# Three halves of RMS-norm factors spread over the partitions by a trip through DRAM instead of four TensorE transposes, in a hybrid attention and gated-MLP layer

## The chip, the cores and the metric

One Trainium2 chip, one core. The metric is the time of one execution in microseconds (us), the median of three runs. The work is spread over TensorE (PE, its weight loads PEld), VectorE (DVE), ScalarE (ACT), GpSimd (POOL) and SyncE (SP). DMAs are issued from two queues, SP's and ACT's; an engine that issues a DMA runs its instructions in order, so a DMA that waits holds what is behind it on that engine.

## The reference

One encoder layer on x of 1024 tokens by 1024 features, all float32:

```python
hn = rmsnorm(h, norm_mix)
qa, ka, va, qb, kb, vb = split(hn @ w_in)
o_a = window_gqa_sink(rope(qa), rope(ka), va, sink)     # |i-j| <= 128, 8 heads, 2 kv heads
o_b = neighbourhood_attention(qb, kb, vb, rpb)          # 8 heads, window 8 x 16 on a 16 x 64 grid
mix = concat(rmsnorm(o_a, norm_a), rmsnorm(o_b, norm_b))
h = h + mix @ w_out
hn = rmsnorm(h, norm_ffn)
h = h + (silu(conv3(hn @ w_gate) + conv_b) * (hn @ w_up)) @ w_down
return rmsnorm(h, norm_final)
```

Here `rmsnorm(y, g) = y * rsqrt(mean(y*y) + eps) * g`, with the mean over the features of one token.

## The kernel before

Activations lie transposed: features on the 128 partitions, tokens along the free dimension, in tiles of 128 by 1024 that are worked on as two halves of 512 tokens (h = 0 and 1; `tsl(h)`). A float32 product is made of three TensorE matmuls over a high and a low part of each operand (`hi` by an ACT copy, `lo` by a DVE subtraction), so every weight and every activation that goes into a product passes once through ACT and once through DVE. The gate and up products of the MLP and its down product each use seven block products in place of eight (names `11`, `12`, `s1` to `s4`, `22`, and `t1` to `t4` for the other operand), and the weights' sums and differences are made on DVE (`ws`).

Since tokens lie along the free dimension, a norm needs one factor per column, equal on all partitions. Squares are added up over the tiles; `inverse_narrow` (or `add_up` and `inverse_root`) transposes the sum on PE, reduces it on DVE to `v`, 128 partitions by 4 columns, one value per token, takes the root on ACT and the reciprocal on DVE. `widen(v, tag)` then turns `v` into a 128 by 512 tile: four PE transposes, each of one column of `v` broadcast to 128 columns, into a PSUM bank `sw`. The product with the factor and the gain is a SCALAR_TENSOR_TENSOR on DVE. The change touches this step at three places, named so in the rest:

- Place A, the norm of attention A's output, second half. `wide_a(1)` at L847 to L851 widens and ACT copies the bank into the tile `rstda`; `normed_a` (L855) multiplies the four tiles `mixa`. These steps are hung on the project job (`aux[...]`) that PE runs between the attention steps.
- Place B, the norm of attention B's output, second half: the loop at L991 to L998, `mixb` times the bank, then the split into `mgh` and `mgl` for the output product.
- Place F, the MLP norm, first half. In the loop over (h, d) of the output product's second part, `inverse_narrow` stands after (1, 1) and `widen` within (1, 3). `settle_out` adds each finished bank to `h1` (DVE, L1063), spills it to DRAM from ACT's queue (`h1d`, L1064), squares it (ACT, L1067) and adds the squares (DVE, L1069). `normed(0, wide, K1)` (L1074) and `operand` (ACT L1050, DVE L1051: the tiles `hg`) make the MLP's operands, first of the tiles K1 = 0 to 3, then of K2 = 4 to 7. The first MLP products `units[0].p1`, `units[1].p1` read K1's, `units[0].p2` reads K2's.

Three things set the order. PE's is the order of the code (`manual_schedule`). On the other engines a scheduler orders the instructions, where `tc.high_priority` draws one forward, `behind(...)` holds one until a marked instruction has been placed, and data dependencies do the rest; each engine then runs its list strictly in order. And the buffers of a pool come free in turn. `head_weights(i, "s2")` (L1083 by `sub`) makes four weight differences `ws` for the first MLP units; nothing but their loads and the scheduler sets their place.

The last norm of the kernel already goes through memory, for its second half: `as_rows` (L1499 to L1503) transposes `v` once to 4 rows of 128, ACT copies them to SBUF, one DMA writes the 2 KB to DRAM and a second reads them back to all 128 partitions.

Of the kernel before, what the change touches and what calls it, by code (L numbers as in the profile page):

```python
# [13 lines left out]
F32 = mybir.dt.float32  # L14
F32R = mybir.dt.float32r
AF = mybir.ActivationFunctionType
ALU = mybir.AluOpType
PSUM = bass.MemoryType.PSUM

D, S, HD = 1024, 1024, 64  # L20
KT = D // 128
NB = S // 128
HALF = 512
# [29 lines left out]
C_NMIX, C_NFFN, C_NFIN, C_NA, C_NB, C_CW, C_CB, C_SINK = 0, 8, 16, 24, 28, 32, 98, 120  # L53
# [5 lines left out]
def hybrid_layer(tc, xT, w_first, w_in, w_out, w_gate, w_up, w_down, small, sink, rpb, consts, rope, out):  # L59
    nc = tc.nc  # L60
    with ExitStack() as ctx:
# [7 lines left out]
        tpool = inner("temps", 3)  # L69
        apool = inner("att", 2)  # L70
        spool = inner("stats", 6)

        slots = {"xg": 16, "op": 14, "mix": 8, "rstd": 1}

        def big(name, tag, dt=F32):
            return lpool.tile([128, S], dt, name=name, tag=tag, bufs=slots[tag])
# [4 lines left out]
        def bank(name, tag):  # L81
            return psum.tile([128, HALF], F32, name=name, tag=tag)

        f32 = lambda ap: ap.bitcast(F32)
        tsl = lambda h: slice(h * HALF, (h + 1) * HALF)
# [4 lines left out]
        col = lambda c: par[:, c:c + 1]  # L90
# [15 lines left out]
        for name, dst, n in (("h", his, 2), ("h", his, 2), ("l", los, 2), ("l", los, 2), ("w", None, 2)):  # L106
            t = flat(big(name, "mix", F32R)[:, :], n)
# [26 lines left out]
        ident = cst[:, K_ID:K_ID + 128]  # L134
# [17 lines left out]
        mark = {}  # L152

        def behind(*names):

            stack = ExitStack()
            for n in names:
                stack.enter_context(tc.issue_after(mark[n].ins))
            return stack
# [23 lines left out]
        def product(ps, ws, xs, h):  # L183

            for i, (w, x) in enumerate(zip(ws, xs, strict=True)):
                block(ps, w, x, h, i == 0, i == len(ws) - 1)
                yield
# [23 lines left out]
        def inverse_narrow(sqs, dim, tag, n=4):  # L211

            ps = bank("ss", tag)
            v = cpool.tile([128, n], F32, name="v4", tag="v4", bufs=4, padded_shape=[128, 4])
            if len(sqs) == 1:
                for c in range(n):
                    nc.tensor.transpose(ps[:, c * 128:(c + 1) * 128], sqs[0][:, c * 128:(c + 1) * 128], ident)
                with tc.high_priority(offset=500):
                    nc.vector.tensor_reduce(v, ps[:, 0:n * 128].rearrange("p (c w) -> p c w", w=128), axis=mybir.AxisListType.X, op=ALU.add)
                    mark["narrow root"] = nc.scalar.activation(v, v, AF.Sqrt, bias=eps, scale=1.0 / dim)  # L220
            else:
                for i, sq in enumerate(sqs):
                    for c in range(n):
                        nc.tensor.matmul(ps[:, c:c + 1], sq[:, c * 128:(c + 1) * 128], ones[:, 0:1], start=c == 0 and i == 0,
                                         stop=i == len(sqs) - 1, skip_group_check=True)
                with tc.high_priority(offset=500):
                    nc.scalar.activation(v[:, 0:n], ps[:, 0:n], AF.Sqrt, bias=eps, scale=float(D) / dim)
            with tc.high_priority(offset=500):
                mark["narrow"] = nc.vector.reciprocal(v[:, 0:n], v[:, 0:n])
            return v  # L230

        def widen(v, tag, n=4):

            wide = bank("sw", tag)
            for c in range(n):
                nc.tensor.transpose(wide[:, c * 128:(c + 1) * 128], v[:, c:c + 1].to_broadcast([128, 128]), ident)
            return wide
# [345 lines left out]
        mg, h1, norm = [None] * 8, [None] * KT, {"halves": 0}  # L583
# [81 lines left out]
        xg, first = [None] * KT, [Project(m) for m in range(3)]  # L665
# [58 lines left out]
        t = quarters(big("f", "mix"))  # L724
# [71 lines left out]
        aux = {}  # L796
# [48 lines left out]
        def wide_a(h):  # L845
            def go():
                if h == 0:  # L847
                    live["op"] += 1
                    norm["a"] = big("rstda", "op")
                with tc.high_priority(offset=500):  # L850
                    nc.scalar.activation(norm["a"][:, tsl(h)], widen(norm["v"][:, 4 * h:4 * h + 4], "pj"), AF.Copy)  # L851
            return go

        def normed_a(i, h):
            return lambda: nc.vector.scalar_tensor_tensor(  # L855
                mix[i][:, tsl(h)], mix[i][:, tsl(h)], col(C_NA + i), norm["a"][:, tsl(h)], op0=ALU.mult, op1=ALU.mult)

        aux[11, 8], aux[12, 2], aux[12, 5], aux[12, 11], aux[12, 13] = square_a, narrow_a, narrow_a, wide_a(0), wide_a(1)
        for i in range(8):
            aux[13, 1 + i + i // 2] = normed_a(*divmod(i, 2))  # L860
        aux[1, KEYS] = second_k
        filler = rest()
        live["op"] = sum(needs(m) for m in range(3))
# [1 line left out]
        def fill(n):  # L865
            while n > 0 and next(filler, False):
                n -= 1
# [3 lines left out]
        for g in range(2):  # L871
            for b in range(NB):
                q, t = unit_window(g, b)
# [59 lines left out]
        for u in range(len(flat)):  # L933
            q, t, need, kind = flat[u]
# [52 lines left out]
        with tc.high_priority(offset=500):  # L987
            vb2 = [inverse_narrow([last[:, tsl(h)]], 512, "pt") for h in range(2)]
        fill(4)
        mg[4:8] = [(big("mgh", "xg", F32R), big("mgl", "xg", F32R)) for _ in range(4)]  # L990
        for h in range(2):  # L991
            wide = widen(vb2[h], "pt")
            for i in range(4):
                x = mix[4 + i][:, tsl(h)]
                hi, lo = (t[:, tsl(h)] for t in mg[4 + i])
                nc.vector.scalar_tensor_tensor(x, x, col(C_NB + i), wide, op0=ALU.mult, op1=ALU.mult)
                nc.scalar.activation(hi, x, AF.Copy)
                nc.vector.tensor_tensor(lo, x, f32(hi), op=ALU.subtract)  # L998
            if h == 0:
                wo = [load_wo(d, True) for d in range(2)]  # L1000
                fill(3)
# [19 lines left out]
        def load_raw(src, n):  # L1021
            raw = fpool.tile([128, n, 128], F32, name="raw", tag="raw", bufs=3, padded_shape=[128, KT, 128])
            nc.sync.dma_start(raw, src)
            return raw
# [9 lines left out]
        def load_half(src):  # L1034

            t = half_raw()
            nc.sync.dma_start(t, src)
            return t
# [16 lines left out]
        K1, K2 = range(0, 4), range(4, 8)  # L1055
        B, W = {}, {}
        late, total = [], [None, None]
        at = lambda k, h: h1[k][:, tsl(h)]
# [12 lines left out]

        def normed(h, wide, ds):
            for d in ds:
                nc.vector.scalar_tensor_tensor(at(d, h), at(d, h), col(C_NFFN + d), wide, op0=ALU.mult, op1=ALU.mult)  # L1074

        def pure(f):
            raw = load_raw(w_gate[f], KT)
# [5 lines left out]
        sub = lambda o, x, y: nc.vector.tensor_tensor(o, x, y, op=ALU.subtract)  # L1083
# [5 lines left out]
        def head_weights(i, name):  # L1089
            f, t = FO[i], wsum[i]  # L1090
            if name == "s1":
                u = load_raw(w_up[f], KT)
                nc.vector.tensor_tensor(t, u[:, 0:4], u[:, 4:8], op=ALU.add)
            elif name == "s2":
                g = load_half(w_gate[f, :, 0:4])
                sub(t, t, g)
            elif name == "s4":
                g = load_half(w_gate[f, :, 4:8])
                sub(t, g, t)
            elif name == "s3":  # L1100
                g, u = load_half(w_gate[f, :, 0:4]), load_half(w_up[f, :, 0:4])
                sub(t, g, u)
            else:
                t = load_half(w_up[f, :, 4:8])
            W[f, name] = split_w(t, 4)

        for h in range(2):
            for d in range(KT):
                if h == 0 and d + 2 < KT:
                    wo.append(load_wo(d + 2, False))  # L1110
                ps = bank("pj", ("o", "s", "pj")[(h * KT + d) % 3])
                for step, _ in enumerate(product(ps, wo[d], mg[4:8], h)):
                    if (h, d, step) == (1, 3, 1):
                        wide = widen(v, "pt")
                late.append((d, h, ps))
                if h == 1 and d == 1:
                    v = inverse_narrow([total[0]], D, "pt")
                settle_out()
                if h == 0 and d in (3, 4):
                    pure((0, FT // 2)[d - 3])  # L1120
                if h == 0 and d >= 5 or h == 1 and d == 0:
                    head_weights((d - 5) % KT, "s1")
                if h == 1 and d == 3:
                    normed(0, wide, K1)
                    B[1, 1] = [operand(at(k, 0), "xg") for k in K1]
                if h == 1 and d == 4:
                    normed(0, wide, K2)
                    B[2, 1] = [operand(at(k, 0), "xg") for k in K2]
# [146 lines left out]
        v = inverse_narrow([total[1]], D, "pt")  # L1275
        units[1].p2()
        wide = widen(v, "pt")
# [194 lines left out]
        sq, todo, vs = {}, [], {}  # L1472
# [75 lines left out]
        for i, (p, j, c) in enumerate(order):  # L1548
# [10 lines left out]
            ps = banks[p, j]  # L1559
# [27 lines left out]
        for k, cols in enumerate(quarters):  # L1587
            for j in (2, 3):
                ps = banks[6, j]
# [17 lines left out]
        first = quarters[1].start  # L1607
# [98 lines left out]
```

## Time and profile before

| | us |
|---|---|
| median of 3 runs (lowest, highest) | 1014.76 (1014.33, 1014.77) |
| the profiled execution, its own time | 1014.52 |
| its span, first to last instruction | 1012.7 |
| PE busy | 1005.1 (99%) |
| DVE busy | 835.0 (82%) |
| ACT busy | 560.7 (55%) |

Times in the trace are counted from the start of the span; 1.8 us of the execution lie outside it. Rows of the timeline give start, duration, engine, line, operation, output and inputs, sizes, and in brackets the idle time of the engine ahead of the row with what ended it. Matmuls are pipelined, so their durations overlap; what one of them costs PE is read from the distance between starts.

### The profile page before, as it was taken

How to read it: one execution, taken by the hardware profiler on the slowest of the kernel's cores; microseconds unless marked ns; L12 is line 12 of the kernel's file. 1: busy time of each engine (PE TensorE's matmuls, PEld its weight loads, DVE VectorE, ACT ScalarE, POOL GpSimd, SP SyncE). 2: the span in 40 equal slices, each digit the busy share in tenths (PEclk: the TensorE clock that was granted, in tenths of full speed). 3: DMA queues.
4: the chain of work that ended last, by engine and by line, in shares of the span. 5: the costliest groups of instructions: out<-in, count | busy, mean ns of one | idle time of the engine just before them, and what ended most of it. 6: DMA issues, size and time to landing. Idle time of an engine off the chain costs nothing.

```text
span 1012.7 us, 14836 instructions
## 1 busy us (share of the span) xinstructions
PE 1005.1 (99%) x5083; PEld 889.5 (88%) x5083; DVE 835.0 (82%) x1570; ACT 560.7 (55%) x1079; POOL 101.9 (10%) x186
## 2 busy tenths in 40 slices
PE   9999999999999999999999999999999999999997
PEld 8899998999899888888888888888888888888887
DVE  7899887768888799999987786786777678996775
ACT  8468776658687554565544443444444645544451
POOL 0224342232232100000000000000000000000001
PEclk9999999999999999999999999999999999999999
DMA  8223122333334366232552333323232699866654
GB/s 295 83 76 92 32 73 63 84 84 84 83 94 136 126 203 222 74 103 64 200 185 92 107 115 115 105 94 119 100 127 84 236 333 318 305 233 238 213 168 177
DMA packets 68372, 145.20 MB, mean 143 GB/s; under 512 B 8260, under 2 KB 18760, under 8 KB 68296
## 3 DMA queue, kind: packets, MB, share of 16 engines
q1 hardware_dynamic: 58216, 119.01, 36.6%
q10 hardware_dynamic: 10080, 25.24, 6.4%
q8 instruction: 40, 0.66, 0.3%
q14 instruction: 36, 0.29, 0.1%
HBM read 103.85 MB, written 28.58 MB: 131 GB/s over the span
## 4 chain that ended last, share of the span: by engine, by line
PE 96%; ACT 1%; DVE 1%; DMA 1%; SPq 0%; issue 0%; DVEq 0%
PE pj L179 8%; PE pj L181 8%; PE pj L180 8%; PE x L1045 8%; PE x L1043 8%; PE x L1044 7%; PE dn L1045 7%; PE dn L1044 7%; PE dn L1043 7%; PE s L393 4%; PE y L1045 4%; PE y L1043 4%; PE y L1044 4%; PE pt L548 2%; PE pt L472 2%; PE z L1043 2%
## 5 line engine op out<-in xcount | busy, mean ns | idle before, releaser
L1043 PE MATMUL x<-hg,whi 128*128 128x512 f32 x352 | 133.5, 379 | 0.0
L1044 PE MATMUL x<-hg,whi 128*128 128x512 f32 x352 | 133.4, 379 | 0.0
L1045 PE MATMUL x<-hg,wlo 128*128 128x512 f32 x352 | 133.4, 379 | 0.0
L1043 PE MATMUL dn<-xd,whi 128*128 128x512 f32 (+1 forms) x330 | 120.8, 366 | 0.0
L1044 PE MATMUL dn<-xd,whi 128*128 128x512 f32 (+1 forms) x330 | 120.5, 365 | 0.0
L1045 PE MATMUL dn<-xd,wlo 128*128 128x512 f32 (+1 forms) x330 | 120.5, 365 | 0.0
L1017 ACT ACTIVATE whi<-ws 128x512 fp32r<-128x512 f32 (+1 forms) x100 | 60.8, 621 | 75.2 <-DVE ws L1157 14.5
L432 ACT ACTIVATE p<-p,nm 128x385 f32<-128x385 f32 (+3 forms) x128 | 75.0, 586 | 45.9 <-DVE nm L424 43.5
L179 PE MATMUL pj<-xgh,whi 128*128 128x512 f32 x245 | 99.7, 407 | 0.0
L436 POOL TENSOR_SCALAR p<-p,sm 128x384 f32<-128x384 f32 (+1 forms) x128 | 75.9, 606 | 195.2 <-DVE sm L434 178.1
L180 PE MATMUL pj<-xgl,whi 128*128 128x512 f32 x245 | 92.9, 379 | 0.0
L181 PE MATMUL pj<-xgh,wlo 128*128 128x512 f32 x245 | 92.9, 379 | 0.0
L1017 ACT ACTIVATE whi<-raw 128x512 fp32r<-128x512 f32 (+1 forms) x102 | 61.0, 611 | 49.9 <-PE x L1044 15.0
L1018 DVE TENSOR_TENSOR wlo<-ws,whi 128x512 fp32r<-128x512 f32 (+1 forms) x100 | 66.7, 680 | 20.0 <-ACT whi L1017 19.7
L447 DVE TENSOR_TENSOR pl<-pt,ph 128x384 fp32r<-128x384 f32 (+2 forms) x108 | 63.4, 587 | 17.1 <-ACT ph L446 16.0
L1043 PEld LDWEIGHTS x<-hg,whi 128*128 128x128 f32 x352 | 66.5, 189 | 9.4
L1044 PEld LDWEIGHTS x<-hg,whi 128*128 128x128 f32 x352 | 66.5, 189 | 9.4
L1045 PEld LDWEIGHTS x<-hg,wlo 128*128 128x128 f32 x352 | 66.5, 189 | 9.4
L1018 DVE TENSOR_TENSOR wlo<-raw,whi 128x512 fp32r<-128x512 f32 (+1 forms) x102 | 66.5, 668 | 5.8 <-ACT whi L1017 5.8
L1518 POOL TENSOR_TENSOR h<-h,wide 128x256 f32<-128x256 f32 x4 | 2.8, 731 | 671.3 <-ACT wide L1514 671.3
L446 ACT ACTIVATE ph<-pt 128x384 fp32r<-128x384 f32 (+2 forms) x108 | 55.3, 512 | 25.7 <-PE pt L472 14.5
L1043 PEld LDWEIGHTS dn<-xd,whi 128*128 128x128 f32 x330 | 62.5, 189 | 7.8
(273 smaller groups left out, 2505.3 us busy)
## 6 DMA issues: line engine op xcount, KB each, us to landing
xd<-x SPq DMA_DIRECT2D x77, 256.0 KB, 4.9
raw<-in_w_down_dram SPq DMA_DIRECT2D x72, 256.0 KB, 4.6
raw<-in_w_gate_dram SPq DMA_DIRECT2D x22, 512.0 KB, 3.5
raw<-in_w_up_dram SPq DMA_DIRECT2D x22, 512.0 KB, 3.7
x<-c ACTq DMA_DIRECT2D x22, 512.0 KB, 2.8
raw<-in_w_in_dram SPq DMA_DIRECT2D x30, 256.0 KB, 2.7
raw<-in_w_down_dram SPq DMA_DIRECT2D x36, 192.0 KB, 4.4
x<-t ACTq DMA_DIRECT2D x11, 512.0 KB, 2.6
```

The source lines that it names most:

```text
L179: nc.tensor.matmul(ps, w[0], mv(x[0][:, tsl(h)]), start=first, stop=False)
L180: nc.tensor.matmul(ps, w[0], mv(x[1][:, tsl(h)]), start=False, stop=False)
L181: nc.tensor.matmul(ps, w[1], mv(x[0][:, tsl(h)]), start=False, stop=last)
L432: nc.scalar.activation(p[:, j, 0:e], p[:, j, 0:e], AF.Exp, bias=nm, scale=-1.0, accum_out=sm[:, j:j + 1])
L436: mark["scaled"] = nc.gpsimd.tensor_scalar(p[:, i, 0:m], p[:, i, 0:m], sm[:, i:i + 1], 1.0, op0=ALU.mult, op1=ALU.mult)
L446: mark["high"] = nc.scalar.activation(ph[:, 0:n], ps[:, 0:n], AF.Copy)
L447: mark["rest"] = nc.vector.tensor_tensor(pl[:, 0:n], ps[:, 0:n], f32(ph[:, 0:n]), op=ALU.subtract)
L1017: nc.scalar.activation(hi, src, AF.Copy)
L1018: nc.vector.tensor_tensor(lo, src, f32(hi[:, :, :]), op=ALU.subtract)
L1043: nc.tensor.matmul(ps, w[0], x[0], start=first and i == 0, stop=False, skip_group_check=True)
L1044: nc.tensor.matmul(ps, w[0], x[1], start=False, stop=False, skip_group_check=True)
L1045: nc.tensor.matmul(ps, w[1], x[0], start=False, stop=last and i == len(ws) - 1, skip_group_check=True)
```

## The change

A new helper does what `as_rows` does, on a DRAM tile of its own: one PE transpose of `v` into 4 rows of 128 in a PSUM bank, an ACT copy into SBUF (`rows`, a corner of a tile that lies unused), a DMA from ACT's queue to DRAM (`roots`), and a DMA back that reads the same 2 KB for each of the 128 partitions into `wide`, from SP's queue at A and B and from ACT's at F. It takes the place of `widen` at the three places. At A the eight multiplications are put in the order of halves, not of tiles. At F the transpose stands behind the last of the four product steps of (1, 2); `widen` stood behind the second step of (1, 3), two steps later. And the third and fourth of the `s2` differences are held behind the fourth multiplication of the MLP norm's first half.

```diff
+        def by_rows(v, rows, wide, tag, read):
+            ps, roots = bank("row", tag), roots_pool.tile([4, 128], F32, name="roots")
+            nc.tensor.transpose(ps[0:4, 0:128], v, ident)
+            with tc.high_priority(offset=500):
+                nc.scalar.activation(rows, ps[0:4, 0:128], AF.Copy)
+                nc.scalar.dma_start(roots, rows)
+                read.dma_start(wide, bass.AP(tensor=roots.tensor, offset=roots.offset, ap=[[0, 128], [1, HALF]]))
...
+                if h == 1:
+                    by_rows(norm["v"][:, 4:8], norm["sq"][0:4, 0:128], norm["a"][:, tsl(1)], "pj", nc.sync)
+                    return
                 with tc.high_priority(offset=500):
-                    nc.scalar.activation(norm["a"][:, tsl(h)], widen(norm["v"][:, 4 * h:4 * h + 4], "pj"), AF.Copy)
+                    nc.scalar.activation(norm["a"][:, tsl(0)], widen(norm["v"][:, 0:4], "pj"), AF.Copy)
...
-            aux[13, 1 + i + i // 2] = normed_a(*divmod(i, 2))
+            aux[13, 1 + i + i // 2] = normed_a(i % 4, i // 4)
...
+        rstd = big("rstdb", "rstd")
         for h in range(2):
-            wide = widen(vb2[h], "pt")
+            if h == 0:
+                wide = widen(vb2[0], "pt")
+                by_rows(vb2[1], rstd[0:4, HALF:HALF + 128], rstd[:, 0:HALF], "pt", nc.sync)
+            else:
+                wide = rstd[:, 0:HALF]
...
+                if (h, d) == (0, K1[-1]):
+                    mark["first normed"] = mark["normed"]
...
-                sub(t, t, g)
+                with behind(*["first normed"] * (i > 1)):
+                    sub(t, t, g)
...
-                    if (h, d, step) == (1, 3, 1):
-                        wide = widen(v, "pt")
+                    if (h, d, step) == (1, 2, 3):
+                        wide = rstd
+                        by_rows(v, wide[0:4, 0:128], wide[:, HALF:S], "pt", nc.scalar)
+                        wide = wide[:, HALF:S]
```

How DVE's list stands at place F, before. In the rows, `ws` is a weight difference, `h1` a tile of the residual stream (an addition from `pj`, or the multiplication by the factor in the bank `sw`), and `s2` the running sum of squares:

```order
L1083 TENSOR_TENSOR ws_4634<-ws_4634,raw_5250 128x512
L1083 TENSOR_TENSOR ws_4635<-ws_4635,raw_5250 128x512
L1069 TENSOR_TENSOR s2_4915<-s2_4915,s2_4897 128x512
L1074 SCALAR_TENSOR_TENSOR h1_3905<-h1_3905,par_76,sw_4925 128x512
L1074 SCALAR_TENSOR_TENSOR h1_4030<-h1_4030,par_76,sw_4925 128x512
L1063 TENSOR_TENSOR h1_4265<-pj_4918,h1_4265 128x512
L1074 SCALAR_TENSOR_TENSOR h1_4141<-h1_4141,par_76,sw_4925 128x512
L1074 SCALAR_TENSOR_TENSOR h1_4265<-h1_4265,par_76,sw_4925 128x512
L1069 TENSOR_TENSOR s2_4938<-s2_4938,s2_4915 128x512
```

And with the change, where the factor is the tile `rstdb` that the DMA fills:

```order
L1103 TENSOR_TENSOR ws_4638<-ws_4638,raw_5255 128x512
L1103 TENSOR_TENSOR ws_4639<-ws_4639,raw_5255 128x512
L1087 TENSOR_TENSOR s2_4925<-s2_4925,s2_4901 128x512
L1081 TENSOR_TENSOR h1_4267<-pj_4928,h1_4267 128x512
L1087 TENSOR_TENSOR s2_4943<-s2_4943,s2_4925 128x512
L1092 SCALAR_TENSOR_TENSOR h1_3907<-h1_3907,par_78,rstdb_4526 128x512
L1081 TENSOR_TENSOR h1_4364<-pj_4962,h1_4364 128x512
L1092 SCALAR_TENSOR_TENSOR h1_4032<-h1_4032,par_78,rstdb_4526 128x512
L1092 SCALAR_TENSOR_TENSOR h1_4143<-h1_4143,par_78,rstdb_4526 128x512
```

The first multiplication has moved two rows back, and the addition of (1, 3)'s bank and the sum of its squares now stand ahead of it, one right behind the other.

ACT's list at the same place, with the change, from the root of `v` on (`h1d` is the spill to DRAM, `s2` here a square):

```order
L230 ACTIVATE v4_4891<-v4_4891,eps_125 128x4
L1082 DMA h1d_4631<-h1_4032 128x512
L78 ACTIVATE rstdb_4526<-row_4917 4x128
L79 DMA roots_4918<-rstdb_4526 4x128
L1085 ACTIVATE s2_4925<-h1_4143 128x512
L1082 DMA h1d_4632<-h1_4143 128x512
L80 DMA rstdb_4526<-roots_4918 128x512
L1085 ACTIVATE s2_4943<-h1_4267 128x512
```

Before, the rows L78 to L80 were not there, and two copies `hg` stood ahead of the last square. The write to DRAM is now queued on ACT's queue behind one spill, and the read back stands between a spill and the next square.

More of the change, by code (lines that the diff above doesn't have):

```diff
@@ L71, in hybrid_layer @@
         spool = inner("stats", 6)
+        roots_pool = ctx.enter_context(tc.tile_pool(name="roots", bufs=1, space=bass.MemoryType.DRAM))
+        def by_rows(v, rows, wide, tag, read):
[5 more added lines that the diff above has]
+                read.dma_start(wide, bass.AP(tensor=roots.tensor, offset=roots.offset, ap=[[0, 128], [1, HALF]]))
         slots = {"xg": 16, "op": 14, "mix": 8, "rstd": 1}
@@ L1073, in normed @@
             for d in ds:
-                nc.vector.scalar_tensor_tensor(at(d, h), at(d, h), col(C_NFFN + d), wide, op0=ALU.mult, op1=ALU.mult)
+                mark["normed"] = nc.vector.scalar_tensor_tensor(at(d, h), at(d, h), col(C_NFFN + d), wide, op0=ALU.mult, op1=ALU.mult)
+                if (h, d) == (0, K1[-1]):
+                    mark["first normed"] = mark["normed"]
         def pure(f):
```

## The prediction

> **What bounds the kernel.** I read the page's busy times and its chain first, then who PE waits for, then the timeline of PE at the three places, and last the timelines of DVE and ACT and the DMA shares there.
>
> ```profile
> PE 1005.1 (99%) x5083; PEld 889.5 (88%) x5083; DVE 835.0 (82%) x1570; ACT 560.7 (55%) x1079; POOL 101.9 (10%) x186
> PE 96%; ACT 1%; DVE 1%; DMA 1%; SPq 0%; issue 0%; DVEq 0%
> ...
> PE sw L236 <- DVE v L229: 0.6, 1, 0.6
> ```
>
> The first row is busy time by engine, the second the chain that ended last, the third the longer of the only two waits that are listed for PE. PE works from end to end, and nearly all of the chain is PE. So an instruction taken from PE at any place is worth its own time, as long as no other engine is then late; and an engine that becomes late there costs what it is late.
>
> **What a transpose costs.** The timeline of PE around `widen` at place F, and around the one existing transpose of the cheaper kind:
>
> ```profile
> 391.25 0.38 PE L181 MATMUL pj<-mgh,wo 128*128 128x512 f32 x1
> 391.47 0.60 PE L236 MATMUL sw<-cst,v 128*128 128x128 f32 x4
> ...
> 392.12 0.38 PE L180 MATMUL pj<-mgl,wo 128*128 128x512 f32 x1
> ...
> 408.74 0.38 PE L1043 MATMUL z<-hg,whi 128*128 128x512 f32 x1
> 408.96 0.38 PE L1044 MATMUL z<-hg,whi 128*128 128x512 f32 x1
> ...
> 986.92 0.38 PE L1045 MATMUL dn<-xd,wlo 128*128 128x512 f32 x1
> 987.14 0.27 PE L1499 MATMUL row<-cst,v 128*4 128x128 f32 x1
> ...
> 987.46 0.38 PE L1044 MATMUL dn<-xd,whi 128*128 128x512 f32 x1
> ```
>
> A plain matmul follows the last by 0.22 us. From 391.25 to 392.12 lie two matmuls (0.43) and four transposes: 0.87 - 0.43 = 0.44, 0.11 each. From 986.92 to 987.46 lie two matmuls and one transpose to rows: 0.54 - 0.43 = 0.11. Each place sheds three transposes, 0.33 us; three places shed 1.0 us. That is the whole of what PE can gain.
>
> **What the trip costs.** The same trip as the last norm makes it now, ACT's copy, the write, the read, and the first use:
>
> ```profile
> 987.45 0.27 ACT L1501 ACTIVATE rows<-row 4x128 f32<-4x128 f32 x1 [2.76 <-PE row L1499]
> 987.74 0.33 SPq L1502 DMA_DIRECT2D spread<-rows  x1
> 988.92 0.35 SPq L1503 DMA_DIRECT2D wide<-spread  x1
> 991.94 1.41 DVE L1520 SCALAR_TENSOR_TENSOR h<-h,par,wide 128x512 f32<-128x512 f32 x2 [0.47 <-DMA wide<-spread]
> ```
>
> From the transpose at 987.14 to the first multiplication it is 4.8 us: 0.6 to the write, 1.2 for the write, 3.0 for the read. The question at each place is when DVE comes to the first multiplication, and what is behind it.
>
> **Places A and B.** DVE at A, then PE, DVE and the DMA share at B (busy times by engine in a stretch, then clock, DMA share and GB/s):
>
> ```profile
> 262.83 0.62 PE L236 MATMUL sw<-cst,v 128*128 128x128 f32 x4
> 262.94 3.39 DVE L855 SCALAR_TENSOR_TENSOR mixa<-mixa,par,rstda 128x512 f32<-128x512 f32 x5
> 269.57 0.56 DVE L447 TENSOR_TENSOR pl<-pt,ph 128x384 fp32r<-128x384 f32 x1
> ...
> 351.95 0.60 PE L236 MATMUL sw<-cst,v 128*128 128x128 f32 x4
> 357.57 1.40 DVE L996 SCALAR_TENSOR_TENSOR mixb<-mixb,par,sw 128x512 f32<-128x512 f32 x2
> 355.00:357.00 2.00, 2.00 (x11) 1.76 (x10) 2.00 (x5) 0.89 (x2) 0.00 (x0) 1.00 0.00 0
> ```
>
> At A, four multiplications with the first half's factor stay where five stood at 262.94, so DVE is 0.67 ahead afterwards; the first with the new factor comes behind the `pl` of 269.57, at 270.1 - 0.67 = 269.4. The transpose at 262.8 and 4.8 us give 267.6; an exponential on ACT may hold the copy for some tenths, 268.2 at the worst that I see. There is a microsecond of cover. At B the row is transposed right behind the first `sw`, at 352.3, ACT is free, the DMA engines are empty from 355, so the factor is there at 357.1; DVE comes to it as the second of the two at 357.57, at 358.2. Again one microsecond. Reading the factor from SBUF costs DVE the same as from the bank (3.39 for five, 1.40 for two). SP issues nothing of weight between, so that it waits for the write is free. If the cover were gone, DVE would stand, and with it the evacuations behind; as the cost without it I take 0 to 1 us at each. Taken: both places give PE their 0.33, 0.66 together.
>
> **Place F.** DVE before, from the weight differences on, and one of ACT's squares:
>
> ```profile
> 392.08 1.35 DVE L1083 TENSOR_TENSOR ws<-ws,raw 128x512 f32<-128x512 f32 x2 [0.98 <-DMA raw<-in_w_gate_dram]
> 393.35 0.68 DVE L1069 TENSOR_TENSOR s<-s,s 128x512 f32<-128x512 f32 x1
> 393.95 1.40 DVE L1074 SCALAR_TENSOR_TENSOR h<-h,par,sw 128x512 f32<-128x512 f32 x2
> 395.26 0.68 DVE L1063 TENSOR_TENSOR h<-pj,h 128x512 f32<-128x512 f32 x1
> 395.98 0.63 ACT L1067 ACTIVATE s<-h 128x512 f32<-128x512 f32 x1
> ...
> 407.62 2.50 DVE L1051 TENSOR_TENSOR hg<-h,hg 128x512 fp32r<-128x512 f32 x4
> 410.03 1.29 DVE L1018 TENSOR_TENSOR wlo<-raw,whi 128x512 fp32r<-128x512 f32 x2
> 411.24 1.29 DVE L1083 TENSOR_TENSOR ws<-ws,raw 128x512 f32<-128x512 f32 x2
> 414.24 0.17 DVE L229 RECIPROCAL v<-v 128x4 f32<-128x4 f32 x1
> ...
> 414.47 0.65 PE L236 MATMUL sw<-cst,v 128*128 128x128 f32 x4
> ```
>
> Before, DVE has no gap from 393.35 to 411. The transpose moves six matmuls ahead of 391.47, to 390.2, so the factor lands at 395.0 in quiet. DVE's list now runs: sum of squares at 393.35, addition of (1, 3)'s bank at 393.95, and right behind it the sum of that addition's square. That one must wait for ACT: an addition started at 395.26, ACT began at 395.98 and took 0.63, so the sum can start 1.40 after the addition and not 0.60, the distance between two such rows. DVE stands for 0.80, a gap that the new order makes by itself. The first multiplication starts at 395.95, 0.95 after the factor. From there the rows are those of before in another order, so the four `hg` of K2 start at 407.62 + 0.80 = 408.42, and the first is done at 409.1. PE wants it for the second matmul of `z`, at 408.96 - 0.33 = 408.6. It waits 0.5, and what F gave is gone. DVE keeps that distance for the next factor: one of the two `ws` at 411.24 moves behind the reciprocal, which takes 0.60 off, so the reciprocal comes 0.2 later than 414.24 and the last `widen` at 414.7 and not at 414.47. Place F then costs 0.2 where it should give 0.33.
>
> The held differences are those two at 411.24; they stood behind the multiplications already, so the hold only keeps them there. Its price is nothing, and without it they could stand in DVE's list ahead of the factor, 1.2 us more in the busy stretch.
>
> **The sum.** A and B give 0.66 and F takes 0.2: 0.46 less, if DVE's chain at F starts as much earlier as PE does. It starts on the landing of weights at 392.08, out of a stretch full of loads that began at 361.44:
>
> ```profile
> 361.44 1.75 SPq L979 DMA_DIRECT2D raw<-in_w_out_dram  x4
> 380.00:384.00 4.00, 4.00 (x20) 3.49 (x19) 3.90 (x7) 1.86 (x3) 0.00 (x0) 1.00 0.94 364
> ```
>
> Where loads set the pace (0.94 of the DMA engines), the start might not move, and then the sum is 0.2 more than before. I take 0.4 less, nearer to the first, since the loads start when PE is done with the projections. From the profiled execution's 1014.52 that is 1014.1; the median of the runs lies 0.24 above that execution, so I say 1014.4. Its own range is 1013.9 to 1015.0. A measurement can tell about 0.2% from no change, 2.0 us here, so this is no change.
>
> **The rivals.** First, all nine transposes are saved: 1.0 less, 1013.8. For it, DVE had 0.65 of slack at `z` before (408.96 against 408.3), so a gap half as long would do no harm. Against it stands the order of the rows.
>
> Second, the factor at F lands late. Two spills from the same queue, one at 388.7 and one at 398.5, from the issue to the landing, and the DMA share around the trip:
>
> ```profile
> L1064 ACTq DMA_DIRECT2D h1d<-h x1: 326/326/326, 388.7 to 388.7; - x1
> ...
> DMA to landing us min/median/max: 4.7/4.7/4.7
> L1064 ACTq DMA_DIRECT2D h1d<-h x1: 326/326/326, 398.5 to 398.5; - x1
> ...
> DMA to landing us min/median/max: 2.0/2.0/2.0
> ...
> 390.00:392.00 2.00, 2.00 (x13) 1.76 (x12) 1.10 (x2) 0.63 (x1) 0.00 (x0) 1.00 0.62 225
> 394.00:396.00 2.00, 2.00 (x11) 1.74 (x10) 2.00 (x5) 1.25 (x3) 0.00 (x0) 1.00 0.70 222
> ```
>
> The spill of 388.7 landed at 393.4, in the busy stretch. If the write, queued on ACT behind it, lands only with it, ACT issues the read at 393.5 and not at 392.0 (390.2, 0.6 to the write, 1.2 for it). With 3.0 to 4.7 for the read the factor lands at 396.5 to 398.2, and each microsecond past 395.95 is a microsecond of PE: 0.5 to 2.2 on the 0.4 less, 1014.9 to 1016.6, around 1015.4. The Trainium skill, page "DMA: Bandwidth & Descriptors", section "Queues, rings and completion order", says that the descriptors of one queue are consumed in ring order on each DMA engine; by that rule this rival is the case, and the sum 0.1 to 1.8 above before. No row here shows it, the trip at 987.74 having had its queue for itself.
>
> Third, and slower: write and read both take the loaded 4.7. Then ACT stands at the read's issue till 395.5, the square of (1, 3) behind it too, and the factor lands at 400.2. That is 4.2 past the slot, 3.8 in the sum: 1018.6. It decides for slower by 0.2% from a landing at 398.4 on; I price it in the middle, 1017.6. For it speaks the 4.7; against it the share falling to 0.62 by 391, and that only 2 KB is written. The Trainium skill, same page, section "Latency and other measured facts", gives HBM access as 0.2 us on average and 2 us at high load, which would work this way; 2.0 against 4.7 for equal spills agrees in direction.
>
> Fourth, the change does less than it says: at A or B the read is late, DVE stands a microsecond, and 0.33 is lost there; 1014.7, within the forecast's range.
>
> **How the numbers follow.** The forecast, with the fourth rival, 0.50; all saved 0.20; late by under 2 us 0.17; slower 0.11; faster by over 2 us 0.02, for which no mechanism is seen, since PE sheds only 1.0. So faster 0.02, same 0.87, slower 0.11. The range runs from 1013.4, all saved less the 0.4 by which the runs before differ, to 1016.6, the end of the second rival.
>
> **What would show it.** In the profile after: one `row` transpose of 0.11 at each place and PE busy down by about 1 us. On DVE at F a gap of 0.8 ahead of the sum of squares, ended by ACT, and no gap ahead of the first multiplication with `rstdb`; a gap there, ended by the DMA, is the second or third rival. On PE a wait of some 0.5 at the first `z` for `hg`. At A and B no gap ahead of `rstda` and `rstdb`. Wrong would be: no wait at `z`, or a wait of PE at a place that I have not named.

## The result and the profile after

The changed kernel takes 1016.74 us (median of 13 runs, 1015.96 to 1018.0) against 1014.76 (13 runs, 1014.33 to 1014.93): 1.0020 times the time before, 95% interval 1.0013 to 1.0027. That is 2.0 us slower where 0.4 less was forecast, and 0.14 past the end of the range. The profiled execution took 1016.41, its span 1014.5 against 1012.7.

The busy times, the chain and three of PE's waits, from the page and the list of waits of the changed kernel:

```profile
PE 1004.5 (99%) x5074; PEld 887.4 (87%) x5074; DVE 835.2 (82%) x1570; ACT 561.4 (55%) x1081; POOL 101.8 (10%) x186
PE 90%; DVE 5%; DMA 3%; ACT 2%; issue 1%; SPq 0%; DVEq 0%; ACTq 0%
...
PE z L1062 <- DVE hg L1069: 1.2, 1, 1.2
...
PE pj L191 <- DVE wo L996: 0.3, 1, 0.3
PE pj L189 <- DVE v L345: 0.3, 1, 0.3
```

PE does nine transposes less and is busy 0.6 us less. But PE has waits that it did not have before: 1.2 us at `z`, 0.3 for a `wo` behind place B, 0.3 for a `v` behind place A (the attention's values, not the norm's). The chain, 96% PE before, now runs for 10% over DVE, the DMA and ACT.

Place F, timelines of ACT, DVE and PE (in the changed kernel the trip is L78 to L80, the sum of squares L1087, the first multiplications L1092, `hg` L1069):

```profile
390.39 0.27 ACT L78 ACTIVATE rstdb<-row 4x128 f32<-4x128 f32 x1 [1.20 <-PE row L76]
390.69 0.27 ACTq L79 DMA_DIRECT2D roots<-rstdb  x1
...
392.28 0.33 ACTq L80 DMA_DIRECT2D rstdb<-roots  x1
...
391.17 1.34 DVE L1103 TENSOR_TENSOR ws<-ws,raw 128x512 f32<-128x512 f32 x2
...
394.42 0.69 DVE L1087 TENSOR_TENSOR s<-s,s 128x512 f32<-128x512 f32 x1 [0.70 <-ACT s L1085]
396.61 0.75 DVE L1092 SCALAR_TENSOR_TENSOR h<-h,par,rstdb 128x512 f32<-128x512 f32 x1 [1.50 <-DMA rstdb<-roots]
...
409.12 2.49 DVE L1069 TENSOR_TENSOR hg<-h,hg 128x512 fp32r<-128x512 f32 x4
...
408.33 0.38 PE L1061 MATMUL z<-hg,whi 128*128 128x512 f32 x1
409.86 0.48 PE L1062 MATMUL z<-hg,whi 128*128 128x512 f32 x1 [1.16 <-DVE hg L1069]
```

The write took 1.6 us (390.69 to the read's issue at 392.28; "write" is counted so in the rest) and the read 4.3 (to 396.61). DVE stood 0.70 ahead of the sum of squares, ended by ACT, and then 1.50 for the factor. Without those 1.50 the four `hg` would have started at 407.62, when they started before.

Behind A PE is there earlier by the 0.30 that it shed and waits for a `v` that DVE does not make earlier by as much; at B the write took 2.2, the read 3.6, and DVE stood 0.49:

```profile
273.68 0.45 PE L189 MATMUL pj<-xgh,whi 128*128 128x512 f32 x1 [0.29 <-DVE v L345]
...
352.65 0.25 ACTq L79 DMA_DIRECT2D roots<-rstdb  x1
...
354.88 0.33 SPq L80 DMA_DIRECT2D rstdb<-roots  x1
...
358.46 0.75 DVE L1014 SCALAR_TENSOR_TENSOR mixb<-mixb,par,rstdb 128x512 f32<-128x512 f32 x1 [0.49 <-DMA rstdb<-roots]
```

Comparing the start of each matmul in both traces shows where PE falls behind or gets ahead; this ledger splits the 1.8 us between the spans: A -0.17 (0.30 shed, 0.31 given back at `v`, 0.18 more shed in two later steps of 0.09), B +0.26 (-0.33, then +0.58 at `wo`), F +1.14 (-0.33, +1.43 at `z`, -0.10, and 0.14 at 498). The rest is at no changed place: -0.18 in the first 31 us, +0.41 at 809, +0.35 behind the last matmul of the ledger.

### The profile page after: what moved, and what is told of

It reads as the page before. It is cut to its first block, busy times and chain, and to the rows that moved or that the text cites. A ratio compares the mean times of both kernels' runs of the same rounds, so it can differ in the third digit from the quotient of the medians.

```text
span 1014.5 us, 14828 instructions
## 1 busy us (share of the span) xinstructions
PE 1004.5 (99%) x5074; PEld 887.4 (87%) x5074; DVE 835.2 (82%) x1570; ACT 561.4 (55%) x1081; POOL 101.8 (10%) x186
## 4 chain that ended last, share of the span: by engine, by line
PE 90%; DVE 5%; DMA 3%; ACT 2%; issue 1%; SPq 0%; DVEq 0%; ACTq 0%
PE x L1061 7%; PE x L1062 7%; PE x L1063 7%; PE pj L189 7%; PE pj L191 7%; PE pj L190 7%; PE dn L1063 6%; PE dn L1061 6%; PE dn L1062 6%; PE y L1062 4%; PE y L1061 4%; PE y L1063 4%; PE s L403 4%; PE pt L482 2%; PE z L1062 2%; PE z L1063 2%
## 5 line engine op out<-in xcount | busy, mean ns | idle before, releaser
L1063 PEld LDWEIGHTS dn<-xd,wlo 128*128 128x128 f32 x330 | 62.5, 189 | 8.2 <-DVE wlo L1036 0.5
```

Source lines behind the costliest of these rows:

```text
L1063: nc.tensor.matmul(ps, w[1], x[0], start=False, stop=last and i == len(ws) - 1, skip_group_check=True)
```

## The experiments

Each kernel was run 11 times (e9 9 times, e8 7) beside before, which took 1014.63 to 1014.80 in the four groups. The intervals of the ratios are 0.0009 wide to each side (e8 and e9 0.001), so the times alone tell apart no less than about 0.9 us; the traces carry the rest.

### Which place loses

Four kernels, each with a part of the change undone: F alone (e1, with the held differences), A alone (e2), B alone (e3), A and B (e4). Where a place is undone, its lines are those of before, and where F is undone the two differences are not held, for instance

```diff
 e2, e3, e4
-                    if (h, d, step) == (1, 2, 3):
-                        wide = rstd
-                        by_rows(v, wide[0:4, 0:128], wide[:, HALF:S], "pt", nc.scalar)
+                    if (h, d, step) == (1, 3, 1):
+                        wide = widen(v, "pt")
...
-                with behind(*["first normed"] * (i > 1)):
-                    sub(t, t, g)
+                sub(t, t, g)
```

> Place F alone goes through memory, with the two differences held; A and B keep their widen. Theory 1 (the changed kernel's loss lies at F, where the factor's trip took 1.6 us for the write and 4.3 for the read in place of 1.2 and 3.0): DVE's first multiplication with the factor again stands over 1 us for the DMA, PE waits for hg at z for 1 us or more, and the time is 1.0 to 1.6 us over before. Rival (the loss is spread: the order of DVE's rows at each place costs, and F pays only the 0.7 us gap ahead of the sum of squares): DVE stands less than 0.5 us for the factor, PE waits 0.5 or less at z, and the time is 0.2 to 0.5 over before.

> Place A alone. Theory 1: no gap ahead of the multiplications with rstda; the 0.33 us that PE sheds is given back by the order of DVE's rows, a v from vt that now stands behind multiplications (PE waited 0.3 us for it in the changed kernel); time within 0.3 us of before. Rival (spread): 0.4 us or more over before, with a gap on DVE or a wait of PE that is not in before.

> Place B alone. In the changed kernel the write took 2.3 us and the read 3.6, the first multiplication with rstdb stood 0.5 us, and PE later waited 0.3 for wo. Theory 1: the same here, the 0.33 that PE sheds is lost again and a little more, 0 to 0.3 us over before. Rival (the late factor at B was chance): no gap ahead of rstdb, no wait of PE, 0.3 under before.

> A and B through memory, F keeps its widen, nothing held. Theory 1 (F makes the loss): 0.3 us under to 0.3 over before, PE's wait for hg at z gone. Rival (spread): 0.7 us or more over before.

| | us | over before | ratio, 95% |
|---|---|---|---|
| F alone | 1015.78 | +1.03 | 1.0002 to 1.0019 |
| A alone | 1013.86 | -0.89 | 0.9983 to 1.0001 |
| B alone | 1013.95 | -0.80 | 0.9986 to 1.0004 |
| A and B | 1014.76 | +0.01 | 0.9992 to 1.0009 |

F alone is the only one whose interval lies above the time before. Its trip, DVE and PE, and the landing of the spill issued ahead of the write:

```profile
390.89 0.51 ACTq L79 DMA_DIRECT2D roots<-rstdb  x1
...
393.50 0.33 ACTq L80 DMA_DIRECT2D rstdb<-roots  x1
...
397.85 0.75 DVE L1085 SCALAR_TENSOR_TENSOR h<-h,par,rstdb 128x512 f32<-128x512 f32 x1 [1.93 <-DMA rstdb<-roots]
...
411.10 0.48 PE L1055 MATMUL z<-hg,whi 128*128 128x512 f32 x1 [1.50 <-DVE hg L1062]
...
L1075 ACTq DMA_DIRECT2D h1d<-h x1: 326/326/326, 388.8 to 388.8; - x1
...
DMA to landing us min/median/max: 4.5/4.5/4.5
```

Here the write took 2.6 and the read 4.3. The spill issued at 388.8 landed at 393.3, and the read, which waits for the write, was issued at 393.5. Theory 1 holds at F. The profiled execution was the second slowest of the eleven (1016.46); in it F costs 2.1 us by the ledger, twice what the median says.

A and B alone in one row each of DVE, with B's trip:

```profile
269.48 0.78 DVE L868 SCALAR_TENSOR_TENSOR mixa<-mixa,par,rstda 128x512 f32<-128x512 f32 x1
```

```profile
352.90 0.51 ACTq L79 DMA_DIRECT2D roots<-rstdb  x1
...
355.24 0.33 SPq L80 DMA_DIRECT2D rstdb<-roots  x1
...
357.48 0.74 DVE L1011 SCALAR_TENSOR_TENSOR mixb<-mixb,par,sw 128x512 f32<-128x512 f32 x1
358.30 0.75 DVE L1011 SCALAR_TENSOR_TENSOR mixb<-mixb,par,rstdb 128x512 f32<-128x512 f32 x1
```

No gap is listed at either. A alone has the wait of 0.3 for `v` again, so its place gives PE -0.19; B alone gives -0.18 at its place. The rows expected for A came, the time expected (within 0.3 of before) not by its median. For B its rival came, no gap and no wait: with write and read at 2.3 and 3.0 the factor at B is just in time, in the changed kernel (2.2 and 3.6) it was half a microsecond late. The two medians of 0.8 to 0.9 under before are more than these places account for in the traces, and together A and B gave nothing; both lie within what these intervals allow.

### What of F's trip is late

```diff
 e6, in by_rows (at F, old is the DRAM tile that B wrote; F writes one of its own)
-                read.dma_start(wide, bass.AP(tensor=roots.tensor, offset=roots.offset, ap=[[0, 128], [1, HALF]]))
+                mark[name] = nc.scalar.dma_start(roots, rows)
+                with behind(*[name] * (old is not None)): read.dma_start(wide, bass.AP(tensor=(old or roots).tensor, ...))
 e7
-                with behind(*["first normed"] * (i > 1)):
+                with behind(*["first normed"] * (i >= 0)):
 e8
-                    if (h, d, step) == (1, 2, 3):
+                    if (h, d, step) == (1, 2, 2):
```

> The changed kernel itself, beside the other runs of this group. A alone and B alone came out 0.8 to 0.9 us under before, both together at before, F alone 1.0 over. If the parts add up, the changed kernel is 1.0 us over before here too; if 2.0 over comes again, something is lost between the places that none of them loses alone.

> The whole change, but at F the read takes the row that B wrote, 40 us earlier, so it does not wait for F's write, and is issued right behind it; the first multiplications are held behind the sum of squares, where they stand in the changed kernel. Left out: the MLP norm's first half is scaled with B's factor. Theory 1 (the factor's landing sets F's loss): the read is issued at about 391.4 in place of 392.3 to 393.5; DVE's wait for it falls from 1.5 to 1.9 us to 0.6 or less, PE's wait at z to 0.9 or less, and the time by 0.7 us or more against the changed kernel. Rival (the order of DVE's rows makes the loss, the wait only fills a gap that would be there): PE's wait at z stays at 1.2 and so does the time.

> The whole change with all four s2 differences held in place of two, which puts the loads of the next weight halves (two of 256 KB, issued 0.3 us behind the read, on SP) later. Theory 1a (the read took 4.3 us because it shares the DMA engines with those loads): the read takes 3.0 to 3.4 us, DVE's wait for the factor is 0.5 us or less, PE's wait at z 0.5 or less. Theory 1b (it took 4.3 for another reason, its queue or its kind): the read takes 4 us or more, DVE waits over 1 us.

> The transpose at F one product step (three matmuls, 0.65 us) earlier; the reciprocal was done 0.7 us ahead of it. Theory 1: the factor lands 0.6 us earlier, DVE's wait and PE's wait at z are 0.6 us shorter, the time 0.6 under the changed kernel. Rival: the write or the read takes longer by as much, because the loads ahead of them are still under way, and nothing changes.

The changed kernel itself (e5) came again at 1016.60, 1.8 over before (1.0007 to 1.0024): the loss is real. Whether it is larger than F's alone, the times cannot tell. The early read, which scales the norm's first half by B's factor, took 1015.56, 1.0 us less than that, as theory 1 had it:

```profile
390.39 0.33 ACTq L80 DMA_DIRECT2D rstdb<-roots  x1
...
394.33 0.69 DVE L1087 TENSOR_TENSOR s<-s,s 128x512 f32<-128x512 f32 x1 [0.70 <-ACT s L1085]
394.94 1.41 DVE L1092 SCALAR_TENSOR_TENSOR h<-h,par,rstdb 128x512 f32<-128x512 f32 x2
...
PE sw L246 <- DVE v L239: 1.0, 2, 0.6
```

The 0.70 in DVE's order is still there, the wait for the factor is gone, and PE has no listed wait for `hg` at `z` (the second matmul there starts 0.53 behind the first, 0.31 more than the step of 0.22). By the ledger PE loses 0.41 at `z` here, against 1.43 in the changed kernel: the wait for the factor makes 1.0 of that, and 0.4 is left with the factor in time, so the order of the rows has its part too. The last line is a wait that the other versions lack: 0.4 more at the last `widen`, where in this kernel both differences stand ahead of the reciprocal on DVE (in the changed kernel one does). Without it the early read would have gained some 0.5 more, an estimate from the ledger (0.49 at `sw`).

With all four differences held (1015.95) no weight load is issued beside the read, and the read took 3.2 with spills on both sides of it. But the write took 2.6, so DVE stood as long as ever:

```profile
390.27 0.27 ACTq L79 DMA_DIRECT2D roots<-rstdb  x1
...
392.91 0.33 ACTq L80 DMA_DIRECT2D rstdb<-roots  x1
...
396.12 0.75 DVE L1092 SCALAR_TENSOR_TENSOR h<-h,par,rstdb 128x512 f32<-128x512 f32 x1 [1.48 <-DMA rstdb<-roots]
```

Theory 1a holds for the read and fails for the arrival. The transpose one step earlier (1017.65) gained nothing, as its rival said:

```profile
390.09 0.27 ACTq L79 DMA_DIRECT2D roots<-rstdb  x1
...
392.43 0.36 ACTq L80 DMA_DIRECT2D rstdb<-roots  x1
...
397.19 0.75 DVE L1092 SCALAR_TENSOR_TENSOR h<-h,par,rstdb 128x512 f32<-128x512 f32 x1 [1.87 <-DMA rstdb<-roots]
```

The write began 0.6 earlier and took 2.3, the read 4.8. In these two traces the write ended no earlier for being issued earlier.

### What the write and the read wait for

```diff
 e9, e11, e12
-                nc.scalar.dma_start(roots, rows)
+                nc.sync.dma_start(roots, rows)
 e10, e11, e13, in settle_out (mark["wide"] is the read in by_rows)
-            nc.scalar.dma_start(spilled[d][:, tsl(h)], at(d, h))
+            todo.append((d, h))
+            if (h, d) != (1, 1):
+                with behind(*["wide"] * ((h, d) == (1, 2))): [nc.scalar.dma_start(spilled[k][:, tsl(g)], at(k, g)) for k, g in todo]
+                todo.clear()
 e13 also
-                with behind(*["first normed"] * (i > 1)):
+                with behind(*["first normed"] * (i >= 0)):
```

In e12 F and the differences are as before.

> The whole change, with the write of the row issued on SP's queue at all three places, as the last norm's trip at 987 does it; nothing else moves on any engine. The last norm's write took 1.2 us from its issue to the read's, the writes from ACT's queue took 2.0 to 2.2 at A and 2.1 to 2.3 at B, where the DMA engines are nearly empty. Theory 2 (the write takes 1.2 from SP and 2 from ACT, whatever else runs): the writes at A and B take 1.2 to 1.4, and the factor at B lands 0.8 us earlier, with no gap ahead of it on DVE. Rival (the 1.2 at 987 belongs to that place): 2.0 or more again. At F, where two weight loads stand ahead of it on SP's queue: 1.6 to 2.6 as from ACT if loads on the ring make it late, and less than 1.6 if only spills on ACT's ring do.

> The whole change, but at F the two spills h1d that were issued ahead of the write (at 388.6) and between write and read (at 391.2) are issued behind the read. Theory 1c (the write stands behind the spill on ACT's ring until that is through, which is the mechanism of the second rival): write 1.2 to 1.4 us, the read issued at about 391.9 in place of 392.3 to 393.5, the factor 0.5 to 1.5 us earlier, the wait at z 0.5 to 1.0 shorter, the time 0.5 under the changed kernel. Rival (it stands behind the weight loads, or writes from ACT take 2 us anyway): write 1.6 to 2.6 as now, no change of time.

> The write on SP's queue at all three places, and the spills at F behind the read. If the two effects add up, the factor at F lands at 394.9 to 396.2, the wait at z is 0 to 0.6, and the time is that of before or up to 0.4 under it, the best that the whole change can give. If the loads alone hold the write, no better than 1.5 us over before.

> A and B through memory with the write on SP's queue, F with its widen as before. By the sums over PE's starts in the runs of A and B alone, 0.2 us under before at each place: 0.4 under before, a little more if B's wait is gone. By the timed run of both together (0.0): no difference.

> The whole change, with both things away from the trip at F that the runs before took away one at a time: the two spills go behind the read, and all four s2 differences are held, so that the next weight loads start later. Theory 1 (the step that failed is the price of 4.8 us for the trip: the write stood behind a spill on its ring, the read beside loads and spills): write 1.2 us, read 3.0 to 3.7, DVE's wait for the factor 0.5 us or less, no wait of PE for hg at z over 0.5, and the time 1.0 to 1.6 us under the changed kernel less the 0.5 us that holding all four costs near 425: 0.2 to 0.9 over before. Rival (the gap in DVE's order alone delays hg): DVE's wait 0.5 or less as well, but PE still waits 1 us at z.

The spills behind the read (e10, 1015.86):

```profile
390.21 0.27 ACTq L79 DMA_DIRECT2D roots<-rstdb  x1
391.39 0.33 ACTq L80 DMA_DIRECT2D rstdb<-roots  x1
391.76 0.45 ACTq L1084 DMA_DIRECT2D h1d<-h  x1
...
391.76 0.80 SPq L1055 DMA_DIRECT2D raw<-in_w_gate_dram  x2
...
396.44 0.75 DVE L1095 SCALAR_TENSOR_TENSOR h<-h,par,rstdb 128x512 f32<-128x512 f32 x1 [1.86 <-DMA rstdb<-roots]
```

The write took 1.2, as theory 1c said. This run alone does not show that it was the spill, since the weight loads were through as well, at 390.44. In the trace's packets the write is four of 512 bytes, about 25 ns each. In e10 they left together at 390.95 to 391.02; in the changed kernel at 391.45 to 391.80; in F alone three by 391.71 and the fourth at 392.96. But the read, now beside one spill and two weight loads issued 0.4 behind it, took 5.0, and what the write gave the read took back: in this trace F costs no less than in the changed kernel.

The write from SP's queue (e9, 1017.15) settles nothing in its favour. At A it took 1.9, at B 2.3, so theory 2 is wrong: the 1.2 at 987 belongs to that place. At F it took 2.7, a little over the 1.6 to 2.6 expected if loads on its own ring made it late, although the spills are on the other queue:

```profile
353.44 0.28 SPq L79 DMA_DIRECT2D roots<-rstdb  x1
355.74 0.35 SPq L80 DMA_DIRECT2D rstdb<-roots  x1
...
391.17 0.27 SPq L79 DMA_DIRECT2D roots<-rstdb  x1
...
393.89 0.33 ACTq L80 DMA_DIRECT2D rstdb<-roots  x1
```

With both (e11, 1016.19) the write at F took 1.2 and the read 3.7, DVE stood 0.38 for the factor, and PE has no listed wait at `z`:

```profile
391.41 0.27 SPq L79 DMA_DIRECT2D roots<-rstdb  x1
...
392.60 0.33 ACTq L80 DMA_DIRECT2D rstdb<-roots  x1
...
396.29 0.75 DVE L1095 SCALAR_TENSOR_TENSOR h<-h,par,rstdb 128x512 f32<-128x512 f32 x1 [0.38 <-DMA rstdb<-roots]
...
359.19 0.75 DVE L1014 SCALAR_TENSOR_TENSOR mixb<-mixb,par,rstdb 128x512 f32<-128x512 f32 x1 [0.80 <-DMA rstdb<-roots]
```

In that profile F costs 0.1 by the ledger, but B's factor was 0.80 late (its write took 2.5), PE then waited 0.5 for `wo`, and the time is not the one expected. A and B from SP (e12, 1015.02, 0.9994 to 1.0012) is inconclusive: no gain of 0.4 shows.

The quiet trip (e13) took 1015.31, 0.7 over before (0.9996 to 1.0015):

```profile
390.94 0.27 ACTq L79 DMA_DIRECT2D roots<-rstdb  x1
392.79 0.33 ACTq L80 DMA_DIRECT2D rstdb<-roots  x1
...
396.22 0.75 DVE L1095 SCALAR_TENSOR_TENSOR h<-h,par,rstdb 128x512 f32<-128x512 f32 x1 [0.89 <-DMA rstdb<-roots]
...
409.47 0.48 PE L1062 MATMUL z<-hg,whi 128*128 128x512 f32 x1 [0.51 <-DVE hg L1069]
```

The write took 1.9 where 1.2 was expected, the read 3.4, PE waited 0.5 at `z`, and the excess is 0.7 in place of 1.8 to 2.0 us. That is theory 1, with DVE's wait 0.4 longer than expected.

The packets tell what the fourth packet of the write stood behind. In the six traces that leave the spills in place and read the row just written (the changed kernel twice, e1, e7, e8, e9) it left 0.2 to 0.7 us after the last packet of the weight loads, while packets of the spills were still running; in e8 it left at 391.93, just as the last packet of the spill issued ahead of it ended (391.94). With the spills behind the read it left with the other three in e10 and e11, though in e11 loads ran until 392.26; in e13 it left at 392.41, right behind the last packet of the loads (392.39). So the spills held it where they were under way, and once loads did.

Laid side by side, DVE's wait for the factor at F and PE's listed wait at `z`, in us: 0 and none (e6), 0.38 and none (e11), 0.89 and 0.5 (e13), 1.48 and 1.1 (e7), 1.50 and 1.2 (the changed kernel), 1.86 and 0.9 (e10), and 1.87, 1.88, 1.80 and 1.93 with 1.5 each (e8, e5, e9, e1; in e10, e9 and e1 another 0.2 to 0.3 falls just ahead of `z`). So DVE can stand about 0.4 before PE has a listed wait, and from there on PE waits about as much longer as DVE does (e10 least).

No version here beats the kernel before by more than the times can tell; A alone comes nearest, 0.9 under, with an interval that reaches 1.0001.

## Why the prediction was wrong

**What PE sheds** was right: 0.33 at B and F (0.44 taken, 0.11 added), 0.30 at A.

**The step that failed** is "so the factor lands at 395.0 in quiet". The 4.8 us were read off a trip at 987 where nothing else was under way, and put into a stretch that the prediction's own rows show busy (0.62 and 0.70 of the DMA engines). Measured there: write 1.6 to 2.7, read 4.2 to 4.8, so the factor came at 396.6 to 398.1 in the kernels that leave the spills and the weight loads where they are. The 0.95 us of cover became a wait of 1.5 to 1.9. In the changed kernel's trace the factor was 1.6 late, which alone would make a wait of 0.7; the rest is that DVE came to the multiplication at 395.1 and not at 395.95, its weight differences having started at 391.17 and not at 392.08. Started earlier, DVE stood longer.

**The second rival** was the case, in its place, its rows and nearly its time (1014.9 to 1016.6): a late factor at F, the landing within 396.5 to 398.2, a gap ahead of the first multiplication ended by the DMA. I had given it 0.17. Its mechanism is shown in part. The write's last packet came behind the spill's (e8), and with the spills behind the read the write took 1.2 (e10, e11). But the spills also held a write from the other queue (e9, 2.7), and loads did so once (e13, 1.9), so it is not only the order within one queue (its ring). The Trainium skill, page "DMA: Bandwidth & Descriptors", section "Queues, rings and completion order", says two things here: on each DMA engine the descriptors of a ring are consumed in ring order, with which e8 agrees, and each DMA engine takes the queues that have work in turn, with which e9, e13 and the slower read beside loads agree. The second half of it, the read, I had bounded by 3.0 to 4.7 and priced at 3.0: 3.2 and 3.4 with spills but no load issued beside it (e7, e13), 4.2 to 4.8 with two loads, 3.7 and 5.0 with a spill and two loads issued behind it (e11, e10). What parts the last two is not shown; the loads followed 0.75 behind the read in e11 and 0.4 in e10.

**The gap of 0.80 in DVE's order** was there, 0.69 to 0.70, in every kernel with F's trip. Its consequence, 0.5 at `z` with the factor in time, was about right: 0.4 by the ledger in e6 and in e11, and F as a whole 0.1 in e11, where the sum had 0.2.

**Places A and B**: "a microsecond of cover" was wrong at B. The trip took 5.2 to 5.5 us from the write's issue there where DVE did not wait, and 5.8 in the changed kernel, where I had 4.2, and the cover was nil. The effect was small as priced in the fourth rival: DVE stood 0 to 0.8 from run to run. At A the factor was in time, but the 0.33 came back as 0.3 at a `v`, a wait that I had not named: PE moved earlier and DVE's chain behind it did not.

**The held differences**, priced at nothing: no run has F without them, so their price is not shown by itself. Holding the other two as well cost 0.2 to 0.5 between 420 and 600 (0.66 in e7 and 0.38 in e13 against 0.14 in the changed kernel).

**What stays open**: in both profiles of the changed kernel the three places make 1.2 to 1.3 us, where the times say 1.8 to 2.0. The remainder sits, in the profiles, in places the change does not touch, and it varies there between executions: +0.41 at 809 in one and 0.00 in another of the same kernel, up to 0.60 in others. Whether the change has a part in that was not tried. So the failed step accounts for F's wait, and not for all of the 2.0 us.

## What to carry to other kernels

The price of a trip through memory depends on what the DMA engines are doing at that place, and is not the one of the place where it was first measured: here 4.2 us from the write's issue in quiet and 5.9 to 7.1 between spills and weight loads, with 4.9 to 6.2 where one or both had been moved. Before moving a factor off PE, look at what is queued when the write is issued and what will be issued right behind the read, and ask for cover by the loaded price, for both transfers. With PE at 99%, a saving of 1.0 us did not bear a wait of 1.5 on DVE.

## What the hardware showed that was not expected

A write of 2 KB in four packets of 25 ns took from 1.2 to 2.7 us until the engine behind it could issue the read, and at F the last of the four made the difference. At B it took 2.2 to 2.5 whichever queue issued it. In the changed kernel's stretch from 350 to 359 the DMA view shows, beside the loads, instructions on their way:

```profile
q8 instruction: 1, 0.02, 1.0%
q14 instruction: 1, 0.01, 0.3%
```

1.0% of 16 engines' 9 us is 1.4 us on one engine. In the packets the one on q14 ran from 353.52 to 353.95, and the fourth packet of the write left at 353.95, 0.53 behind the third. The same stands in every trace with B's trip, twelve in all: three packets of the write leave together, a packet of instructions on q14 follows, and the fourth leaves within 4 ns of its end, 0.44 to 0.67 behind the third. At 987 before, no packet of instructions was near, and the four left within 0.06. So at B the write stood behind a load of instructions, though the packets do not name their DMA engine and no run moved that load. That is about half of what the write took there above 1.2. The other half lies behind the fourth packet: from its end to the read's issue it is 0.85 to 1.03 at B and 0.34 at 987, and the cause of that stays open.
